# Gate and up projections of a decoder layer: stationary weights with 256 token columns moving, against stationary tokens with 512 weight columns moving

## The chip, the cores and the metric

The kernel runs on one core of a Trainium2 chip. The core has a matrix engine (TensorE, PE in the profile; its weight loads are PEld), a vector engine (VectorE, DVE), an activation engine (ScalarE, ACT), GpSimd (POOL), a queue engine (SyncE, SP), and DMA engines that move data between HBM and the on-chip memory SBUF. Matmul results land in PSUM, in 8 banks of 512 float32 columns on 128 partitions. The metric is device time of the whole launch in microseconds; lower is better.

## The reference, cut to what matters

One layer of a hybrid decoder on 256 tokens (plus 16 meta tokens), model width 2048, in float32. After the token mixers comes a SwiGLU feed-forward with hidden width 5632:

```python
def channel_mixing(h, w_gate_up, w_down, g_pre, g_post):
    xn = rmsnorm(h, g_pre)
    gu = jnp.einsum('bld,df->blf', xn, w_gate_up)
    gate, up = gu[..., :FFN_HIDDEN], gu[..., FFN_HIDDEN:]
    y = jnp.einsum('blf,fd->bld', jax.nn.silu(gate) * up, w_down)
    return rmsnorm(y, g_post)
```

Ahead of it stand the in-projection (2048 to 5132 columns), mLSTM, stick-breaking and pooling mixers, and the out-projection (2048 to 2048) with its norm and residual.

## The kernel before, in words

All large products run in a split form: each float32 operand is written as `hi` (rounded to the matrix engine's one-pass format fp32r) and `lo` (the rest), and a product is three matmuls, hi·hi, hi·lo and lo·hi. Weights are streamed from HBM in chunks of 1 MB into one of three `raw` buffers (`load`, L82); ScalarE makes `hi` (L93), VectorE makes `lo` (L94), each in two pieces of 1024 columns, into four `hi` and four `lo` buffers (`split`, L88). Loads are issued on SyncE's queue as a raw buffer comes free. A matmul has a stationary operand of 128x128 and a moving one of up to 512 columns. The program stands in the order in which the source issues it, and a scheduler then orders each engine's instructions by readiness and priority.

The stages, in order: in-projection (weights stationary, up to 272 token columns moving); out-projection in two halves (`ktile_product`, tokens stationary, 512 weight columns moving, L626 to L628); the first group of gate and up (512 gate and 512 up columns, `fg_part`, L738, tokens stationary, 512 columns moving, L744 to L746); ten more groups of gate and up (L826 to L851); the down projection in two halves (`ktile_product` again).

In those ten groups the weights are stationary and the 256 token columns `x2hi`, `x2lo` move (`mm3`, L97). A group has four blocks of 128 hidden columns, a PSUM bank each, gate in the left half and up in the right. The loop runs over four chunks `c` of 4 k tiles and over `s` (gate, up). The results have hidden channels on the partitions and tokens in the columns, which is what the down projection needs as its stationary operand. Each block is scaled by the second norm's factor per token column, `rb2`, and multiplied (L848 to L851) into float32 tiles `ha`, `hb`, `hc`. `rb2` is made in `norm2` with two float32 matmuls (L726). The first group has tokens on the partitions, so it uses the norm factor as a per-partition scalar (L769, L770) and is turned by eight TensorE transposes (L823) ahead of group 2.

In the down projection `lhs_h` (L868) splits each hidden k tile again, once per half, into `hh` and `hl` from a pool of six each (L872, L873).

Of the kernel before, what the change touches and what calls it, by code (L numbers as in the profile page):

```python
# [18 lines left out]
P = 128  # L19
D = 2048  # L20
# [17 lines left out]
def tile_hybrid_layer(  # L38
# [22 lines left out]
    cst = ctx.enter_context(tc.tile_pool(name="cst", bufs=1))  # L61
    wp = ctx.enter_context(tc.tile_pool(name="wp", bufs=1))
# [113 lines left out]
    # gate weights, input gate columns at 0..5 and forget gate columns at 32..37  # L176
# [290 lines left out]
    def tick():  # L467
        # one block's worth of matmuls has been issued: let one waiting step follow, if its input has had time
# [68 lines left out]
    def first(kind, i):  # L537
        # first token that a block is needed for
# [8 lines left out]
    def load_group(ka, kb, blocks):  # L547
        nb = len(blocks)
        starts = [base[kind] + P * i for kind, i in blocks]
        raw = wp.tile([P, 2 * MB], F32, tag="raw", name=nm("raw"), bufs=RAWB)  # L550
# [68 lines left out]
    mhi, mlo_ = mix_tiles()  # L619

    def ktile_product(wview, nk, half, accs, lhs, on_block, ticks=False, before_tail=None):
        # accs[i][j]: token tile i, 512-column block j of this half; the last four k tiles go block by block
# [8 lines left out]
        for ci in range(0, nk, 2):  # L631
# [3 lines left out]
            if ci + 4 < nk:  # L635
# [28 lines left out]
    def post_evac(accs, i, cb, yt, gt, ss):  # L664
# [4 lines left out]
        if cb == 2:  # L669
            # the mean square of the blocks so far, and EPS  # L670
# [17 lines left out]
    fp = ctx.enter_context(tc.tile_pool(name="fp", bufs=1))  # L688
    exst = ExitStack()
    ex = exst.enter_context(tc.tile_pool(name="ex", bufs=4))  # L690
    h2 = fp.tile([P, 2, D], F32, name="h2")
    gpost = fp.tile([P, D], F32, tag="gpost", name="gmp")
    act.dma_start(out=gpost, in_=g_mix_post.broadcast_to([P, D]))
    act.dma_start(out=h2, in_=x_v)
    yg = fp.tile([P, 2, D], F32, tag="yg", name="yg")
# [16 lines left out]
    rb2 = fp.tile([P, NT], F32, name="rb2")  # L712

    def norm2():
# [16 lines left out]
    fg_split, later = {}, []  # L731

    def fg_load(c, where=None):
        for s in range(2):
            r = load(gu_view(c * 4, s * HID), 4, 512)
            fg_split[s, c] = [(c * 4 + 2 * j, split(r[:, 2 * j : 2 * j + 2], 2, 512, where)) for j in range(2)]

    def fg_part(s, c, i):  # L738
        ts = slice(i * P, (i + 1) * P)
        for k0, (h, l) in fg_split[s, c]:  # L740
            for kk in range(2):
                k = k0 + kk
                o = fg_banks[s][i]
# [3 lines left out]

    fg_banks = []

    def fg_begin():  # L750
        four = [mx() for _ in range(4)]
        fg_banks.extend([four[s], four[s + 2]] for s in range(2))
        for s in range(2):
            fg_part(s, 0, 0)

    def fg_rest():
        for s in range(2):
            fg_part(s, 0, 1)
        norm2()
        exst.close()  # L760
        for c in range(1, 4):
            fg_load(c)
            for s in range(2):
                for i in range(2):
                    fg_part(s, c, i)
                    if c == 3 and s == 1:
                        sc = rr[:, 1, i : i + 1]
                        hg = fp.tile([P, 512], F32, tag="hg", name=nm("hg"), bufs=2)
                        act.activation(hg, fg_banks[0][i], AF.Silu, scale=sc)  # L769
                        vec.scalar_tensor_tensor(out=hg, in0=fg_banks[1][i], scalar=sc, in1=hg,  # L770
                                                 op0=ALU.mult, op1=ALU.mult)
                        later.append((i, hg))
# [7 lines left out]
    def finish_mix(i, j):  # L780
# [30 lines left out]
    ha = big.tile([P, 16, NT], F32, tag="mixhi", name="ha")  # L811
    hb = big.tile([P, 16, NT], F32, tag="mixlo", name="hb")
    hc = fw.tile([P, 12, NT], F32, tag="hc", name="hc", bufs=1)

    def hid(f):
        return ha[:, f, :] if f < 16 else hb[:, f - 16, :] if f < 32 else hc[:, f - 32, :]


    def first_group_end():
        for i, hg in later:  # L820
            pt = mx()
            for b in range(4):
                pe.transpose(pt[:, b * P : (b + 1) * P], hg[:, b * P : (b + 1) * P], ident)  # L823
            act.copy(out=ha[:, 0:4, i * P : (i + 1) * P], in_=pt.rearrange("p (a b) -> p a b", b=P))

    for gi in range(1, 11):  # L826
        if gi == 2:
            first_group_end()
        banks = [mx() for _ in range(4)] if gi % 2 == 0 else [acc(b) for b in range(4)]
        for c in range(4):  # L830
            for s in range(2):
                r = load(gu_view(c * 4, s * HID + gi * 512), 4, 512)
                subs = [(c * 4 + 2 * j, split(r[:, 2 * j : 2 * j + 2], 2, 512)) for j in range(2)]
                last = c == 3
                if last:
                    its = [(k0, kk, h, l, b) for b in range(4) for k0, (h, l) in subs for kk in range(2)]
                else:
                    its = [(k0, kk, h, l, b) for k0, (h, l) in subs for b in range(4) for kk in range(2)]
                for k0, kk, h, l, b in its:
                    k = k0 + kk  # L840
                    bs = slice(b * P, (b + 1) * P)
                    mm3(banks[b][:, s * NT : (s + 1) * NT], h[:, kk, bs], l[:, kk, bs], x2hi[:, k, :], x2lo[:, k, :],
                        k == 0 and s == 0, k == KT - 1, skip_group_check=True)
                    if last and s == 1 and k == KT - 1:
                        f = gi * 4 + b
                        t1 = fw.tile([P, NT], F32, tag="t1", name=nm("t1"))
                        t2 = fw.tile([P, NT], F32, tag="t2", name=nm("t2"))
                        vec.tensor_tensor(out=t1, in0=banks[b][:, :NT], in1=rb2, op=ALU.mult)  # L848
                        act.activation(t1, t1, AF.Silu)
                        vec.tensor_tensor(out=t2, in0=banks[b][:, NT:], in1=rb2, op=ALU.mult)  # L850
                        vec.tensor_tensor(out=hid(f), in0=t1, in1=t2, op=ALU.mult)  # L851

# [1 line left out]
    gpost2 = fp.tile([P, D], F32, tag="gpost", name="gfp")  # L854
    sp.dma_start(out=gpost2, in_=g_ffn_post.broadcast_to([P, D]))
# [66 lines left out]
```

## Time and profile before

| | |
|---|---|
| time, median of 3 runs | 1154.13 us (1154.11 to 1154.23) |
| span of the profiled execution | 1154.4 us |
| PE busy | 1143.4 us, 99%, 7795 matmuls |
| PEld busy | 1058.6 us, 92% |
| DVE, ACT busy | 677.2 us (59%), 519.4 us (45%) |
| DMA | 208.84 MB, mean 181 GB/s |

The profiled execution is one run of the program; its span, 1154.4 us, is 0.3 us over the median of the timed runs. A matmul's listed duration reaches from its start to a modelled end and contains its way through the array, so that several overlap; what a matmul costs is read from the distance between the starts of consecutive ones.

### The profile page before, as it was taken

The page shows a single profiled execution, that of the slowest core. Times are in us where ns is not written, and L with a number is a line of the kernel's source. Part 1 is how long each engine was busy: PE and PEld are TensorE (multiplying, and loading weights), DVE is VectorE, ACT ScalarE, POOL GpSimd, SP SyncE. Part 2 cuts the span into 40 slices and gives each one's busy share as a digit, 9 for nine tenths or more (in the row PEclk, how much of TensorE's full clock was granted, in tenths as well). Part 3 has the DMA queues.
Part 4 walks back from the last instruction along what each step waited for, and adds up shares of the span by engine and source line. Part 5 has one row for each costly group of instructions (what it writes and reads, how often), then busy time and mean ns, then how long its engine had stood idle before and what let it go on. Part 6 is the DMA issues. An engine that isn't in the chain of part 4 may idle for free.

```text
span 1154.4 us, 18718 instructions
## 1 busy us (share of the span) xinstructions
PE 1143.4 (99%) x7795; PEld 1058.6 (92%) x7795; DVE 677.2 (59%) x936; ACT 519.4 (45%) x759; POOL 23.0 (2%) x65
## 2 busy tenths in 40 slices
PE   9999999999999999999999999999999999999997
PEld 7999999999888789999999999999999888878885
DVE  4777655759945845645455365454453765565555
ACT  6544445534444844434334344343343544454442
POOL 4000000000000000000000000000000000000000
PEclk8999999999999999999999999999999999999999
DMA  7554543555465565455555554555555555555551
GB/s 237 179 181 149 188 146 114 170 147 170 167 273 219 183 208 193 167 188 184 179 189 183 185 183 167 202 183 177 190 183 184 185 182 183 183 187 193 195 190 73
DMA packets 100565, 208.84 MB, mean 181 GB/s; under 512 B 3962, under 2 KB 31402, under 8 KB 99952
## 3 DMA queue, kind: packets, MB, share of 16 engines
q1 hardware_dynamic: 99312, 202.63, 51.2%
q10 hardware_dynamic: 416, 3.15, 0.6%
q0 software_dynamic: 752, 1.87, 0.6%
q8 instruction: 61, 1.00, 0.4%
q14 instruction: 24, 0.20, 0.0%
HBM read 205.52 MB, written 2.11 MB: 180 GB/s over the span
## 4 chain that ended last, share of the span: by engine, by line
PE 98%; DVE 1%; DMA 0%; ACT 0%; issue 0%; SPq 0%; DVEq 0%; POOLq 0%; ACTq 0%
PE acc L100 14%; PE acc L98 14%; PE acc L99 14%; PE mx L98 7%; PE mx L100 7%; PE mx L99 7%; PE mx L627 5%; PE acc L627 5%; PE mx L628 5%; PE mx L626 5%; PE acc L628 5%; PE acc L626 5%; PE mx L744 1%; PE mx L746 1%; PE mx L745 1%; PE mx L327 0%
## 5 line engine op out<-in xcount | busy, mean ns | idle before, releaser
L94 DVE TENSOR_TENSOR lo<-raw,hi 128x1024 fp32r<-128x1024 f32 (+1 forms) x384 | 458.6, 1200 | 363.4 <-ACT hi L93 361.4
L93 ACT CAST hi<-raw 128x1024 fp32r<-128x1024 f32 (+1 forms) x384 | 391.7, 1029 | 398.4 <-PE acc L99 210.1
L100 PE MATMUL acc<-xhi,lo 128*128 128x272 f32 (+4 forms) x640 | 192.4, 301 | 0.0
L98 PE MATMUL acc<-xhi,hi 128*128 128x272 f32 (+4 forms) x640 | 187.7, 293 | 0.6 <-DVE im L292 0.4
L99 PE MATMUL acc<-xlo,hi 128*128 128x272 f32 (+4 forms) x640 | 187.1, 292 | 0.0
L98 PE MATMUL mx<-x2hi,hi 128*128 128x256 f32 x640 | 181.3, 283 | 0.0
L99 PE MATMUL acc<-x2lo,hi 128*128 128x256 f32 x640 | 181.1, 283 | 0.0
L100 PE MATMUL acc<-x2hi,lo 128*128 128x256 f32 x640 | 181.1, 283 | 0.0
L98 PE MATMUL acc<-x2hi,hi 128*128 128x256 f32 x640 | 181.1, 283 | 0.0
L99 PE MATMUL mx<-x2lo,hi 128*128 128x256 f32 x640 | 181.1, 283 | 0.0
L100 PE MATMUL mx<-x2hi,lo 128*128 128x256 f32 x640 | 181.1, 283 | 0.0
L98 PEld LDWEIGHTS acc<-xhi,hi 128*128 128x128 f32 x640 | 121.8, 190 | 2.7 <-issue 1.4
L100 PEld LDWEIGHTS acc<-xhi,lo 128*128 128x128 f32 x640 | 121.7, 190 | 1.6 <-issue 1.0
L98 PEld LDWEIGHTS mx<-x2hi,hi 128*128 128x128 f32 x640 | 122.9, 192 | 0.1
L99 PEld LDWEIGHTS acc<-x2lo,hi 128*128 128x128 f32 x640 | 122.9, 192 | 0.0
L98 PEld LDWEIGHTS acc<-x2hi,hi 128*128 128x128 f32 x640 | 122.9, 192 | 0.0
L100 PEld LDWEIGHTS acc<-x2hi,lo 128*128 128x128 f32 x640 | 122.9, 192 | 0.0
L99 PEld LDWEIGHTS mx<-x2lo,hi 128*128 128x128 f32 x640 | 122.9, 192 | 0.0
L100 PEld LDWEIGHTS mx<-x2hi,lo 128*128 128x128 f32 x640 | 122.9, 192 | 0.0
L99 PEld LDWEIGHTS acc<-xlo,hi 128*128 128x128 f32 x640 | 121.8, 190 | 0.5 <-DVE xlo L215 0.2
L627 PE MATMUL mx<-lo,hh 128*128 128x512 f32 x176 | 69.7, 396 | 0.0
L627 PE MATMUL acc<-lo,hh 128*128 128x512 f32 x176 | 69.6, 396 | 0.0
(246 smaller groups left out, 1390.8 us busy)
## 6 DMA issues: line engine op xcount, KB each, us to landing
raw<-in_w_gate_up_dram SPq DMA_DIRECT2D x88, 1024.0 KB, 4.9
raw<-in_w_down_dram SPq DMA_DIRECT2D x44, 1024.0 KB, 4.9
raw<-in_w_in_dram SPq DMA_DIRECT2D x36, 512.0 KB, 4.7
raw<-in_w_out_dram SPq DMA_DIRECT2D x16, 1024.0 KB, 5.0
raw<-in_w_in_dram SPq DMA_DIRECT2D x12, 1024.0 KB, 5.1
raw<-in_w_in_dram SPq DMA_DIRECT2D x8, 768.0 KB, 4.3
raw<-in_w_in_dram SPq DMA_DIRECT2D x3, 792.0 KB, 6.9
h<-in_x_dram ACTq DMA_DIRECT2D x1, 2048.0 KB, 11.9
```

What stands on the lines that cost most here:

```text
L93: act.copy(out=h, in_=r)
L94: vec.tensor_tensor(out=l, in0=r, in1=h.bitcast(F32), op=ALU.subtract)
L98: pe.matmul(o, lhsT=wh, rhs=xh, start=start, stop=False, **kw)
L99: pe.matmul(o, lhsT=wh, rhs=xl, start=False, stop=False, **kw)
L100: pe.matmul(o, lhsT=wl, rhs=xh, start=False, stop=stop, **kw)
L626: pe.matmul(o, lhsT=lh, rhs=h[:, 0, js], start=k == 0, stop=False)
L627: pe.matmul(o, lhsT=lh, rhs=l[:, 0, js], start=False, stop=False)
L628: pe.matmul(o, lhsT=ll, rhs=h[:, 0, js], start=False, stop=k == nk - 1)
L744: pe.matmul(o, lhsT=x2hi[:, k, ts], rhs=h[:, kk, :], start=k == 0, stop=False)
L745: pe.matmul(o, lhsT=x2hi[:, k, ts], rhs=l[:, kk, :], start=False, stop=False)
L746: pe.matmul(o, lhsT=x2lo[:, k, ts], rhs=h[:, kk, :], start=False, stop=k == KT - 1)
```

## The change

All eleven groups now run as the first one did: tokens stationary, 512 weight columns moving (`gu_part`), gate and up for each of the two token tiles in a bank of their own. `gu_evac` takes Silu of the gate bank with the norm factor as scale and multiplies it with the up bank into `hg`, tokens on partitions. After the next group's first chunk, `hidden_out` transposes a group's `hg` by eight TensorE transposes into two spare banks, ScalarE copies them out as `hi`, VectorE writes `lo`; these stay in SBUF (`hidhi`, `hidlo`), and `lhs_h` only picks slices. `rb2` and its matmuls are gone. The last group's transposes stand in the down projection after its first chunk of weights.

The second part is where tiles lie in SBUF. Pools stack from the low end in the order in which they are opened; `rawp` and `ft` (for `hg`) are now on the right side, at the high end. Counted from the tiles' sizes, in KB (1024 bytes) of a partition:

| tiles | before | after |
|---|---|---|
| raw | 17 to 41 | 200 to 224 |
| hi, lo (weights) | 41 to 57, 57 to 73 | 17 to 33, 33 to 49 |
| x2hi, x2lo (and xhi, xlo) | 73 to 90, 90 to 107 | 49 to 66, 66 to 83 |
| mixhi, mixlo (out-projection) | 107 to 123, 123 to 139 | 83 to 99, 99 to 115 |
| hi, lo of the first group's first chunk | 186 to 202, 202 to 218 | 157 to 173, 173 to 189 |
| stationary tiles of down, hi | hh 206 to 212 | groups 0 to 3: 83 to 99, 4 to 10: 133 to 161 |
| stationary tiles of down, lo | hl 212 to 218 | groups 0 to 3: 99 to 115, 4 to 10: 161 to 189 |

The core of the diff:

```diff
+    rawp = ctx.enter_context(tc.tile_pool(name="rawp", bufs=1, side="right"))
...
-        raw = wp.tile([P, 2 * MB], F32, tag="raw", name=nm("raw"), bufs=RAWB)
+        raw = rawp.tile([P, 2 * MB], F32, tag="raw", name=nm("raw"), bufs=RAWB)
...
-        pr = acc(3)
-        for i in range(2):
-            dg = fp.tile([P, P], F32, tag="dg", name=nm("dg"))
-            vec.tensor_scalar(out=dg, in0=ident, scalar1=rr[:, 1, i : i + 1], scalar2=None, op0=ALU.mult)
-            pe.matmul(pr[:, i * P : (i + 1) * P], lhsT=ones, rhs=dg, start=True, stop=True)
-        vec.tensor_copy(out=rb2, in_=pr[:, :NT])
...
+    def gu_part(banks, s, i, subs):
+        ts = slice(i * P, (i + 1) * P)
+        for k0, (h, l) in subs:
+            for kk in range(2):
+                k = k0 + kk
+                o = banks[s][i]
+                pe.matmul(o, lhsT=x2hi[:, k, ts], rhs=h[:, kk, :], start=k == 0, stop=False)
+                pe.matmul(o, lhsT=x2hi[:, k, ts], rhs=l[:, kk, :], start=False, stop=False)
+                pe.matmul(o, lhsT=x2lo[:, k, ts], rhs=h[:, kk, :], start=False, stop=k == KT - 1)
+
+    def gu_evac(banks, i):
+        sc = rr[:, 1, i : i + 1]
+        hg = ft.tile([P, 512], F32, tag="hg", name=nm("hg"))
+        act.activation(hg, banks[0][i], AF.Silu, scale=sc)
+        vec.scalar_tensor_tensor(out=hg, in0=banks[1][i], scalar=sc, in1=hg, op0=ALU.mult, op1=ALU.mult)
+        return hg
...
+        for i, hg in enumerate(hgs):
+            pt = bank(i)
+            for b in range(4):
+                pe.transpose(pt[:, b * P : (b + 1) * P], hg[:, b * P : (b + 1) * P], ident)
+            p4 = pt.rearrange("p (a b) -> p a b", b=P)
+            ts = slice(i * P, (i + 1) * P)
+            act.copy(out=hidden[0][gi][:, :, ts], in_=p4)
+            vec.tensor_tensor(out=hidden[1][gi][:, :, ts], in0=p4, in1=hidden[0][gi][:, :, ts].bitcast(F32),
+                              op=ALU.subtract)
...
-    for gi in range(1, 11):
-        if gi == 2:
-            first_group_end()
-        banks = [mx() for _ in range(4)] if gi % 2 == 0 else [acc(b) for b in range(4)]
-        for c in range(4):
...
-                    mm3(banks[b][:, s * NT : (s + 1) * NT], h[:, kk, bs], l[:, kk, bs], x2hi[:, k, :], x2lo[:, k, :],
-                        k == 0 and s == 0, k == KT - 1, skip_group_check=True)
...
+    for gi in range(11):
+        banks = fg_banks if gi == 0 else four(gi)
+        hgs = []
+        for c in range(1 if gi == 0 else 0, 4):
             for s in range(2):
+                subs = gu_load(c, gi, s)
+                if c == 3:
+                    for i in range(2):
+                        gu_part(banks, s, i, subs)
+                        if s == 1:
+                            hgs.append(gu_evac(banks, i))
                 else:
+                    for sub in subs:
+                        for i in range(2):
+                            gu_part(banks, s, i, [sub])
+            if c == 0:
+                hidden_out(gi - 1, later, spare(gi - 1))
+        later = hgs
...
-                act.copy(out=hh, in_=hid(k))
-                vec.tensor_tensor(out=hlo, in0=hid(k), in1=hh.bitcast(F32), op=ALU.subtract)
...
+            return hidden[0][k // 4][:, k % 4, ts], hidden[1][k // 4][:, k % 4, ts]
```

Two smaller edits go with it: the last norm's gain `gfp` is loaded on POOL's queue into the space of `x2lo` (before: on SyncE's queue into a tile of its own), and the last result tile `yg2` lies in the space of `x2hi`.

PE, before, where the first group's transposes stand between group 1 (banks `acc`) and group 2 (banks `mx`); the names are output bank, then moving and stationary operand:

```order
L98 MATMUL acc_575_4481<-x2hi_3746,hi_614_4894 128x256
L99 MATMUL acc_575_4481<-x2lo_3747,hi_614_4894 128x256
L100 MATMUL acc_575_4481<-x2hi_3746,lo_615_4895 128x256
L823 MATMUL mx_624_4970<-ident_72,hg_570_4454 128x128 x4
L823 MATMUL mx_625_4976<-ident_72,hg_571_4469 128x128 x4
L98 MATMUL mx_626_4982<-x2hi_3746,hi_631_4988 128x256
L99 MATMUL mx_626_4982<-x2lo_3747,hi_631_4988 128x256
```

PE, after, at the end of group 1's first chunk; eight transposes of the group ahead stand here, and the same again in each later group and once in the down projection:

```order
L738 MATMUL acc_572_4479<-hi_581_4520,x2hi_3755 128x512
L739 MATMUL acc_572_4479<-lo_582_4521,x2hi_3755 128x512
L740 MATMUL acc_572_4479<-hi_581_4520,x2lo_3756 128x512
L764 MATMUL mx_583_4550<-ident_75,hg_567_4458 128x128 x4
L764 MATMUL mx_584_4557<-ident_75,hg_568_4473 128x128 x4
L738 MATMUL acc_569_4476<-hi_586_4566,x2hi_3755 128x512
L739 MATMUL acc_569_4476<-lo_587_4567,x2hi_3755 128x512
```

The weights have gone from the second place (stationary) to the first (moving), and one matmul of 512 columns does what two of 256 did. Up to the first group's second chunk the order on PE is the same in both programs.

VectorE, after, at the end of group 0 and the start of group 1 (the `lo` rows are pieces of group 1's weights; the two `hg` rows read group 0's up banks for token tiles 0 and 1):

```order
L96 TENSOR_TENSOR lo_575_4483<-raw_573_4480,hi_574_4482 128x1024
L96 TENSOR_TENSOR lo_577_4487<-raw_573_4480,hi_576_4486 128x1024
L746 SCALAR_TENSOR_TENSOR hg_567_4458<-mx_519_4124,rr_3737,hg_567_4458 128x512
L96 TENSOR_TENSOR lo_580_4517<-raw_578_4514,hi_579_4516 128x1024
L746 SCALAR_TENSOR_TENSOR hg_568_4473<-mx_520_4125,rr_3737,hg_568_4473 128x512
L96 TENSOR_TENSOR lo_582_4521<-raw_578_4514,hi_581_4520 128x1024
```

Three of the next group's four `lo` pieces stand ahead of the second `hg` row, which waits for the group's last matmul.

## Rows read from the trace of the kernel before

**Rows 1.** Busy time by stage: us, then PE, PEld, DVE, ACT, POOL; clock; DMA share; GB/s.

```profile
299.70:391.30 91.60, 91.25 (x409) 74.63 (x408) 58.21 (x79) 44.21 (x63) 0.56 (x1) 1.00 0.65 241
409.80:437.80 28.00, 28.00 (x125) 23.21 (x125) 13.28 (x13) 12.88 (x13) 0.00 (x0) 1.00 0.53 181
437.80:899.60 461.80, 461.80 (x3849) 461.65 (x3848) 236.54 (x284) 182.13 (x207) 0.00 (x0) 1.00 0.53 183
899.60:1146.60 247.00, 246.97 (x1058) 197.56 (x1056) 148.14 (x188) 119.48 (x183) 0.54 (x1) 1.00 0.50 177
1146.60:1154.40 7.80, 0.00 (x0) 0.00 (x0) 3.50 (x6) 0.69 (x2) 0.54 (x1) 0.84 0.44 162
```

**Rows 2.** The chain of work that ended last, by engine.

```profile
PE 98%; DVE 1%; DMA 0%; ACT 0%; issue 0%; SPq 0%; DVEq 0%; POOLq 0%; ACTq 0%
```

**Rows 3.** Timeline of PE in the ten groups: start us, us; nine steps apart.

```profile
559.80 0.28 PE L98 MATMUL acc<-x2hi,hi 128*128 128x256 f32 x1
...
560.88 0.28 PE L98 MATMUL acc<-x2hi,hi 128*128 128x256 f32 x1
```

**Rows 4.** Timeline of PE in the first group's later chunks, nine steps apart.

```profile
423.78 0.39 PE L745 MATMUL mx<-lo,x2hi 128*128 128x512 f32 x1
...
425.82 0.39 PE L745 MATMUL mx<-lo,x2hi 128*128 128x512 f32 x1
```

**Rows 5.** The same, where its first chunk ends and the second begins.

```profile
402.80 0.40 PE L746 MATMUL mx<-hi,x2lo 128*128 128x512 f32 x1
...
404.43 0.40 PE L744 MATMUL mx<-hi,x2hi 128*128 128x512 f32 x1
404.66 0.39 PE L745 MATMUL mx<-lo,x2hi 128*128 128x512 f32 x1
...
406.48 0.39 PE L744 MATMUL mx<-hi,x2hi 128*128 128x512 f32 x1
```

**Rows 6.** Timeline of PE in the down projection, nine steps apart.

```profile
999.74 0.40 PE L626 MATMUL acc<-hi,hh 128*128 128x512 f32 x1
...
1001.84 0.39 PE L626 MATMUL acc<-hi,hh 128*128 128x512 f32 x1
```

**Rows 7.** Timeline of PE around the first group's transposes.

```profile
483.91 1.03 PE L823 MATMUL mx<-ident,hg 128*128 128x128 f32 x8
484.70 0.36 PE L98 MATMUL mx<-x2hi,hi 128*128 128x256 f32 x1
484.90 0.28 PE L99 MATMUL mx<-x2lo,hi 128*128 128x256 f32 x1
```

**Rows 8.** Line 823 by itself: duration ns min/median/max, first and last start.

```profile
L823 PE MATMUL mx<-ident,hg x8: 271/272/273, 483.9 to 484.7; 128*128 128x128 f32 x8
```

**Rows 9.** Timeline of PE around four transposes among 512-column products.

```profile
387.19 0.60 PE L798 MATMUL acc<-ident,h 128*128 128x128 f32 x4
387.55 0.48 PE L626 MATMUL mx<-hi,mixhi 128*128 128x512 f32 x1
387.87 0.60 PE L798 MATMUL acc<-ident,h 128*128 128x128 f32 x4
```

**Rows 10.** Timeline of PE around the second norm's matmuls.

```profile
408.75 0.38 PE L726 MATMUL acc<-dg,ones 128*128 128x128 f32 x2
...
409.58 0.49 PE L726 MATMUL acc<-dg,ones 128*128 128x128 f32 x2
...
410.14 0.39 PE L745 MATMUL mx<-lo,x2hi 128*128 128x512 f32 x1
```

**Rows 11.** Groups on ACT and DVE: busy us, mean ns, idle before.

```profile
L93 ACT CAST hi<-raw 128x1024 fp32r<-128x1024 f32 x352 | 365.4, 1047 | 369.4 <-PE acc L99 187.3 <-PE mx L99 119.9 <-PE mx L628 19.7
L769 ACT ACTIVATE hg<-mx,rr 128x512 f32<-128x512 f32 x2 | 1.4, 690 | 0.0
L94 DVE TENSOR_TENSOR lo<-raw,hi 128x1024 fp32r<-128x1024 f32 x352 | 428.3, 1223 | 347.1 <-ACT hi L93 346.6
L770 DVE SCALAR_TENSOR_TENSOR hg<-mx,rr,hg x2: 745/745/745, 435.5 to 438.9; 128x512 f32<-128x512 f32 x2
```

More of the change, by code (lines that the diff above doesn't have):

```diff
@@ L549, in load_group @@
         starts = [base[kind] + P * i for kind, i in blocks]
-        raw = wp.tile([P, 2 * MB], F32, tag="raw", name=nm("raw"), bufs=RAWB)
+        raw = rawp.tile([P, 2 * MB], F32, tag="raw", name=nm("raw"), bufs=RAWB)
         r = raw[:, : (kb - ka) * nb * P].rearrange("p (k c) -> p k c", c=nb * P)
@@ L642, in ktile_product @@
                 pend = []
+            if ci == 0 and after_first:
+                after_first()
         if before_tail:
@@ L688, in tile_hybrid_layer @@
     fp = ctx.enter_context(tc.tile_pool(name="fp", bufs=1))
+    ft = ctx.enter_context(tc.tile_pool(name="ft", bufs=4, side="right"))
     exst = ExitStack()
+    yp = exst.enter_context(tc.tile_pool(name="yp", bufs=1))
     ex = exst.enter_context(tc.tile_pool(name="ex", bufs=4))
     h2 = fp.tile([P, 2, D], F32, name="h2")
-    gpost = fp.tile([P, D], F32, tag="gpost", name="gmp")
+    gpost = yp.tile([P, D], F32, name="gmp")
     act.dma_start(out=gpost, in_=g_mix_post.broadcast_to([P, D]))
     act.dma_start(out=h2, in_=x_v)
-    yg = fp.tile([P, 2, D], F32, tag="yg", name="yg")
+    yg = yp.tile([P, 2, D], F32, name="yg")
     ssy = fp.tile([P, 2, 4], F32, name="ssy")
@@ L709, in gu_view @@
         return w_gu[0, k0 * P : (k0 + 4) * P, c0 : c0 + 512].rearrange("(k p) c -> p k c", p=P)
-    rb2 = fp.tile([P, NT], F32, name="rb2")
     def norm2():
@@ L721, in norm2, with gu_load @@
             inv_rms(rr[:, 1, i : i + 1], s1, 1)
-        pr = acc(3)
-        for i in range(2):
-            dg = fp.tile([P, P], F32, tag="dg", name=nm("dg"))
-            vec.tensor_scalar(out=dg, in0=ident, scalar1=rr[:, 1, i : i + 1], scalar2=None, op0=ALU.mult)
-            pe.matmul(pr[:, i * P : (i + 1) * P], lhsT=ones, rhs=dg, start=True, stop=True)
-        vec.tensor_copy(out=rb2, in_=pr[:, :NT])
[L731 to L738, printed above, removed]
+    def gu_load(c, gi, s, where=None):
+        r = load(gu_view(c * 4, s * HID + gi * 512), 4, 512)
+        return [(c * 4 + 2 * j, split(r[:, 2 * j : 2 * j + 2], 2, 512, where)) for j in range(2)]
+    def gu_part(banks, s, i, subs):
         ts = slice(i * P, (i + 1) * P)
-        for k0, (h, l) in fg_split[s, c]:
+        for k0, (h, l) in subs:
             for kk in range(2):
                 k = k0 + kk
-                o = fg_banks[s][i]
+                o = banks[s][i]
                 pe.matmul(o, lhsT=x2hi[:, k, ts], rhs=h[:, kk, :], start=k == 0, stop=False)
@@ L746, in fg_part, with hidden_out @@
                 pe.matmul(o, lhsT=x2lo[:, k, ts], rhs=h[:, kk, :], start=False, stop=k == KT - 1)
-    fg_banks = []
+    def gu_evac(banks, i):
[4 more added lines that the diff above has]
+        return hg
+    hidden = []
+    def hidden_out(gi, hgs, bank):
+        if gi < 8 and gi % 4 == 0:
+            for s in ("hi", "lo"):
+                if gi == 0:
+                    q = big.tile([P, 16, NT], F32R, tag=f"mix{s}", name=f"hid{s}")
+                    hidden.append([q[:, 4 * g : 4 * g + 4] for g in range(4)])
+                else:
+                    q = hp.tile([P, 28, NT], F32R, name=f"hid{s}2")
+                    hidden[s == "lo"] += [q[:, 4 * g : 4 * g + 4] for g in range(7)]
+        for i, hg in enumerate(hgs):
[7 more added lines that the diff above has]
+                              op=ALU.subtract)
@@ L750, in fg_begin, with four, spare @@
+    fg_split, later = {}, []
+    fg_banks = []
+    def four(gi):
+        f = [mx() for _ in range(4)] if gi % 2 == 0 else [acc(b) for b in range(4)]
+        return [f[0:2], f[2:4]]
+    def spare(gi):
+        return (lambda i: mx()) if gi % 2 == 0 else acc
     def fg_begin():
-        four = [mx() for _ in range(4)]
-        fg_banks.extend([four[s], four[s + 2]] for s in range(2))
+        fg_banks.extend(four(0))
         for s in range(2):
-            fg_part(s, 0, 0)
+            gu_part(fg_banks, s, 0, fg_split[s])
@@ L756, in fg_rest @@
     def fg_rest():
         for s in range(2):
-            fg_part(s, 0, 1)
+            gu_part(fg_banks, s, 1, fg_split[s])
         norm2()
         exst.close()
[L761 to L772, printed above, removed]
@@ L804, in finish_mix @@
                                          in1=x2hi[:, k, ts].bitcast(F32), op0=ALU.mult, op1=ALU.subtract)
-    ktile_product(wout_view, KT, 1, accs1, lhs_mix, done, before_tail=lambda: fg_load(0, ex))
+    ktile_product(wout_view, KT, 1, accs1, lhs_mix, done, before_tail=lambda: fg_split.update((s, gu_load(0, 0, s, ex)) for s in range(2)))
     fg_rest()
-    fw = ctx.enter_context(tc.tile_pool(name="fw", bufs=4))
-    ha = big.tile([P, 16, NT], F32, tag="mixhi", name="ha")
-    hb = big.tile([P, 16, NT], F32, tag="mixlo", name="hb")
@@ L813, in tile_hybrid_layer @@
[L813 to L824, printed above, removed]
-    for gi in range(1, 11):
-        if gi == 2:
-            first_group_end()
-        banks = [mx() for _ in range(4)] if gi % 2 == 0 else [acc(b) for b in range(4)]
-        for c in range(4):
-            for s in range(2):
[L832 to L836, printed above, removed]
-                else:
[L838 to L841, printed above, removed]
-                    mm3(banks[b][:, s * NT : (s + 1) * NT], h[:, kk, bs], l[:, kk, bs], x2hi[:, k, :], x2lo[:, k, :],
-                        k == 0 and s == 0, k == KT - 1, skip_group_check=True)
[L844 to L851, printed above, removed]
@@ L854, in tile_hybrid_layer @@
-    gpost2 = fp.tile([P, D], F32, tag="gpost", name="gfp")
-    sp.dma_start(out=gpost2, in_=g_ffn_post.broadcast_to([P, D]))
-    yg2 = fp.tile([P, 2, D], F32, tag="yg", name="yg2")
+    hp = ctx.enter_context(tc.tile_pool(name="hp", bufs=1))
+    for gi in range(11):
+        banks = fg_banks if gi == 0 else four(gi)
+        hgs = []
+        for c in range(1 if gi == 0 else 0, 4):
+            for s in range(2):
+                subs = gu_load(c, gi, s)
[4 more added lines that the diff above has]
+                            hgs.append(gu_evac(banks, i))
+                else:
+                    for sub in subs:
[4 more added lines that the diff above has]
+        later = hgs
@@ L857, in tile_hybrid_layer @@
+    gpost2 = big.tile([P, KT * T], F32, tag="xlo", name="gfp")[:, :D]
+    pool.dma_start(out=gpost2, in_=g_ffn_post.broadcast_to([P, D]))
+    yg2 = big.tile([P, KT * T], F32, tag="xhi", name="yg2")[:, : 2 * D].rearrange("p (i d) -> p i d", d=D)
     ssz = fp.tile([P, 2, 4], F32, name="ssz")
@@ L865, in tile_hybrid_layer, with lhs_h @@
         accs = [flat[0:2], flat[2:4]]
-        hl = {}
-        def lhs_h(k, i, hl=hl):
-            if k not in hl:
-                hh = fw.tile([P, NT], F32R, tag="hh", name=nm("hh"), bufs=6)
-                hlo = fw.tile([P, NT], F32R, tag="hl", name=nm("hl"), bufs=6)
-                act.copy(out=hh, in_=hid(k))
-                vec.tensor_tensor(out=hlo, in0=hid(k), in1=hh.bitcast(F32), op=ALU.subtract)
-                hl[k] = (hh, hlo)
+        def lhs_h(k, i):
             ts = slice(i * P, (i + 1) * P)
-            return hl[k][0][:, ts], hl[k][1][:, ts]
+            return hidden[0][k // 4][:, k % 4, ts], hidden[1][k // 4][:, k % 4, ts]
         def done2(i, j, half=half, accs=accs):
@@ L890, in finish_ffn @@
                 sp.dma_start(out=out_v[:, i, cs], in_=yg2[:, i, cs])
-        ktile_product(wd_view, NF, half, accs, lhs_h, done2)
+        last = (lambda: hidden_out(10, later, spare(10))) if half == 0 else None
+        ktile_product(wd_view, NF, half, accs, lhs_h, done2, after_first=last)
 _INS = ['x', 'meta_tokens', 'w_in', 'ml_conv_w', 'ml_igate_b', 'ml_fgate_b', 'pool_w', 'pool_scale', 'w_out',
```

2 lines of the change are left out of this document (1 added, 1 removed).

## The prediction

> **What bounds the kernel now.** I read the busy times by stage first. In the ten groups of gate and up PE is busy for 461.80 of 461.80 us, in the down projection for 246.97 of 247.00, in the out-projection for 91.25 of 91.60, while DVE and ACT are busy for 237 and 182 us of the 461.8 [rows 1]. Then the chain that ended last: PE has 98% of it [rows 2]. So PE never waits for data in the stages that the change touches, and their length is the number of matmuls times the distance between two starts. That distance is the number to read; the listed 0.28 and 0.39 us of one matmul overlap.
>
> The timeline gives it. 256 moving columns: nine steps in 560.88 - 559.80 = 1.08 us, 120 ns each [rows 3]. The stage agrees: (461.8 us - 0.87 for the eight transposes inside it) / 3840 products = 120.0 ns. 512 columns in the first group: nine steps in 425.82 - 423.78 = 2.04 us, 226.7 ns [rows 4]. 512 in the down projection: 1001.84 - 999.74 = 2.10 us, 233.3 ns [rows 6], and the stage 247.0 / 1056 = 233.9. At the granted clock of 1.00 in these stages [rows 1], the 2.4 GHz level, 512 columns are 213.3 ns and 256 are 106.7. So each matmul pays a fixed 13.3 ns in both of the first cases, whichever of weights and tokens is stationary, and 20 ns in the down projection.
>
> Where do the other 6.7 ns come from? In the first group the first chunk's `hi` and `lo` lie at 186 to 218 KB, the later chunks' at 41 to 73. Between 402.80 and 404.43 seven steps take 233 ns each; from 404.66, the second matmul that reads the low buffers, to 406.48 eight take 227.5 [rows 5]. Same instructions, same stationary tiles; the place of the moving tile is what differs. In the down projection it is the stationary tile that lies high (206 to 218 KB), with all else at or below 73. The out-projection, with stationary tiles at up to 139 KB, is a 512-column stage without the high ones. I take it that an operand high in SBUF costs 6.7 ns per matmul. One switch carries this, so it stays a reading.
>
> **The ten groups' products.** 10 groups x 2 (gate, up) x 4 blocks x 16 k tiles x 3 = 3840 matmuls become 10 x 2 x 2 token tiles x 16 x 3 = 1920. New operands lie at 17 to 49 and 49 to 83 KB. 3840 x 120.0 = 460.9 us; 1920 x 226.7 = 435.3. Change: -25.6 us, all on the path. If the high spacing came instead, 1920 x 233.3 = 447.9: -13.0.
>
> The Trainium skill, "TensorE: Matmul & The Clock Gate", section "Back-to-back issue gap", gives the distance of two matmuls at the full clock as N/2.4 + 2.5 ns. By it a fixed part of 2.5 ns would be saved 1920 times, an estimate of 4.8 us. Rows 3 and 4 show 13.3 in its place, and the sum goes by them.
>
> **The transposes.** 80 more on PE (8 for each of groups 1 to 10; group 0's were there). Nothing hides them: PE is the bound. Eight took 483.91 to 484.70, and the product behind them had a step of 0.20 us for 0.12 [rows 7]: 0.79 + 0.08 = 0.87 us. Among 512-column products four took 0.36 and the next step 0.32 for 0.23 [rows 9], 0.45 us; eight in one piece are then 8 x 0.099 + 0.09 = 0.88. 10 x 0.87 = +8.7 us. After such an interruption some ten steps run nearer to 233 than to 227 (the same is seen behind the norm's matmuls): 10 x 0.04 = +0.4. Lower end 8.4, upper 10 x 0.45 x 2 plus twice that tail, 9.8.
>
> A single transpose is listed with 272 ns [rows 8], and they start 99 ns apart. The Trainium skill, same page, section "Part 4: PE-mode transpose", has about 275 ns for one in a kernel. The duration agrees with that; taken as a cost, 80 of them would be an estimate of 22 us, but the path pays the spacing [rows 7].
>
> They wait for `hg`, which needs Silu and one multiply after the group's last matmul, 0.69 + 0.745 us [rows 11], and they stand 48 matmuls, 10.9 us, behind it. So no wait is added there.
>
> **The norm's matmuls.** From 408.75 to 410.14, 1.39 us, PE does four float32 matmuls and three products [rows 10]; three products alone are 0.68. Change: -0.7.
>
> **The down projection.** 1056 matmuls, 233.9 ns now. All low: 1056 x 6.9 = -7.3. Only k tiles 0 to 15 certainly low (83 to 115 KB): 16/44 of that, -2.6. Unknown is the stretch between 139 KB, the highest low tile seen, and 186, the lowest high one. `hidhi` of the later groups, 133 to 161, is nearer to the first, `hidlo`, 161 to 189, to the second. `lo` of 28 k tiles is read by 28 x 8 = 224 matmuls; the other 832 x 6.9 = -5.7. I take that. If the 20 ns came instead from the waits on `hh` and `hl`, which also go, it would be -7.3; if from something that stays, 0.
>
> **Costed at nothing.** DVE: per group 16 operations on 256 columns become two multiplies of 0.745 us and two subtractions on 512; per 1024-column piece of weights it has 1.22 us of work [rows 11] against 12 x 0.227 = 2.72 us of PE time, ACT 1.05. The `lhs_h` work of the down projection goes; both were covered. The one new wait that could reach PE is on DVE: the multiply for token tile 1 waits for the group's last matmul, with the fourth `lo` piece of the next group behind it. That piece is ready 0.745 + 1.22 = 2.0 us after the group's end and is wanted after three pieces, 8.2 us. The copies of a transposed group wait on ACT and DVE for PE's transposes, with splits behind them that are wanted a chunk, 5.4 us, later. Loads: PE now eats 1 MB in 24 x 0.227 = 5.4 us for 5.8, 193 GB/s for 183; the out-projection ran 241 [rows 1]. The `gfp` load moves from SP's queue, where weight loads stood behind it, to POOL's, where it waits for the last read of `x2lo` with only the final norm's two powers behind it, and is wanted 120 us later. In-projection and out-projection move down by 24 KB inside the low stretch: 0. The first chunk of the first group, 48 matmuls, moves from 186 to 218 to 157 to 189: 0, at most -0.3. The tail of 7.8 us [rows 1] keeps its work.
>
> **Sum.** -25.6 + 8.7 + 0.4 - 0.7 - 5.7 = -22.9 us. The profiled execution's span of 1154.4 becomes 1131.5; it stands 0.3 over the median, so the time is 1131.2 us.
>
> **Rivals.**
> - *The gain is in the ten groups alone.* The down projection keeps 233 ns, because what is high there is not what costs, or the boundary lies just over 139 KB: -17.2 to -19.8, 1134 to 1137 us. For it: the boundary has not been seen. Against: the sharp switch in rows 5. 18%.
> - *The spacing is 233 everywhere.* The extra 6.7 ns then belongs to something the change carries into the ten groups. 1131.2 + 12.9 + 5.7 = 1149.8. Against: 227 for the same instruction on the same stationary tiles [rows 4]. 8%.
> - *PE waits at every group boundary.* All `lo` pieces of the next group come late behind the new multiply: 0.745 + 1.22 = 2.0 us each, after which DVE's 1.22 per piece outruns PE's 2.72. 10 x 2.0: 1151. Against: the order has three pieces ahead of it. 3%.
> - *Slower: the fixed part is small and the transposes outweigh it.* The place is the stream of products: halving their number gives back only the fixed part, 1920 times, and the transposes cost 9.1. The point from which it decides is 9.1/1920 = 4.7 ns. If 512 columns cost twice what 256 do (240 ns), halving gives back nothing, and with the down projection as it was the time is 1154.1 + 9.1 - 0.7 = 1162.5 us. Against it stand rows 3 and 4, 13.3 ns in both forms [rows 3, 4]. 4%. The rule of the Trainium skill's "TensorE: Matmul & The Clock Gate" cited above lies on this side of the point: its 2.5 ns would make an estimate of 1157.7.
> - *A further step lower.* Operands below 41 KB save another 6.7 ns in the in-projection (1920 matmuls), out-projection (384) and gate and up (2112): -29.6, 1102 us. For it: the step from 20 to 13.3. Against: 13.3 is the same with tiles at 41 and at 139 KB. 3%.
>
> **How the numbers follow.** Forecast 64%: 1131.2, by its bounds (down -7.3 to -2.6, transposes 8.4 to 9.8) 1129 to 1135. With the first rival 82%, so the range is 1126 to 1141: at the low end all of the down projection (-1.6) and 3.5 us for stages costed at nothing, at the high end no gain there (1137) and 4 us more for transposes or short waits. 0.2%, 2.3 us, is what a measurement of this kernel can tell from no change. Faster: 64 + 18 + 3, 7 of the 8 and 2 of the 3: 94%. Same: 2%. Slower: 4%.
>
> **What would show it.** PE timeline in groups 1 to 10: steps of 226.7 ns, eight transposes at 0.87 us once a group, no wait of PE on DVE or ACT; gate and up from group 1 on about 444 us. In the down projection, steps of 227 for k tiles 0 to 15, and from 16 on 227 for the two matmuls that hold `hidhi` and about 233 for the one with `hidlo`. In-projection unchanged to 0.5 us. The prediction is wrong where the 512-column steps in the ten groups differ from 227 by more than 3 ns, or where PE shows waits of over 0.5 us per group.

## The result, and the profile after

The changed kernel takes 1134.97 us, median of 4 runs (1134.61 to 1135.14), against 1154.18 us for the kernel before (1154.11 to 1154.6). The ratio is 0.9834, 95% interval 0.9822 to 0.9846: 19.2 us less, where 22.9 were forecast (1131.2 us).

Busy time by stage in the kernel after: out-projection, first group, ten groups, down projection, end. Columns as in [rows 1].

```profile
298.16:389.65 91.49, 91.14 (x408) 74.56 (x407) 58.10 (x79) 43.95 (x63) 0.56 (x1) 1.00 0.68 241
389.65:435.43 45.78, 45.78 (x209) 37.47 (x208) 28.18 (x52) 28.34 (x59) 2.53 (x3) 1.00 0.45 142
435.43:879.70 444.27, 444.27 (x2002) 368.65 (x2000) 220.49 (x201) 189.93 (x200) 0.00 (x0) 1.00 0.58 190
879.70:1124.80 245.10, 245.10 (x1065) 198.42 (x1063) 114.45 (x105) 94.33 (x101) 1.14 (x2) 1.00 0.55 183
1124.80:1132.90 8.10, 0.17 (x1) 0.00 (x0) 3.50 (x6) 0.69 (x2) 0.54 (x1) 0.79 0.45 166
```

PE is busy for all of the three changed stages, as before [rows 1]. Against before, from the first matmul of each to the first of the next stage (the last one: to one step behind its last matmul), the ten groups went from 461.80 to 444.27 us, the first group from 46.54 to 45.78, the down projection from 246.76 to 245.11 with eight transposes more in it, the out-projection from 91.53 to 91.49.

All waits of PE in the kernel after: who waited, for what, us in total, times, longest.

```profile
PE mx L212 <- DMA mt<-in_meta_tokens_dram: 1.7, 1, 1.7
PE mx L188 <- DVE ssx L200: 1.1, 1, 1.1
PE acc L100 <- DVE im L294: 0.4, 1, 0.4
PE acc L817 <- issue: 0.4, 1, 0.4
```

None stands in the ten groups or the down projection (L212, L188, L100 are the in-projection, L817 the turning of the out-projection's result). Now the starts of consecutive matmuls. PE in the ten groups of the kernel after, nine steps apart, then around one group's transposes (start us, us, engine, line, tile, shape):

```profile
560.10 0.39 PE L739 MATMUL acc<-lo,x2hi 128*128 128x512 f32 x1
...
562.14 0.39 PE L739 MATMUL acc<-lo,x2hi 128*128 128x512 f32 x1
```

```profile
446.32 1.03 PE L764 MATMUL mx<-ident,hg 128*128 128x128 f32 x8
447.11 0.48 PE L738 MATMUL acc<-hi,x2hi 128*128 128x512 f32 x1
447.42 0.39 PE L739 MATMUL acc<-lo,x2hi 128*128 128x512 f32 x1
```

2.04 us / 9 = 226.7 ns, the spacing of [rows 4] carried to all groups. The eight transposes take 0.79, the next step 0.31 for 0.23: 0.87 us, as [rows 7] gave. PE in the down projection of the kernel after, in the third block of four k tiles and in the fifth, nine steps each:

```profile
902.37 0.39 PE L628 MATMUL acc<-hi,hidhi 128*128 128x512 f32 x1
...
904.40 0.39 PE L628 MATMUL acc<-hi,hidhi 128*128 128x512 f32 x1
...
924.13 0.39 PE L628 MATMUL acc<-hi,hidhi 128*128 128x512 f32 x1
...
926.23 0.40 PE L628 MATMUL acc<-hi,hidhi 128*128 128x512 f32 x1
```

2.03 / 9 = 226 ns for k tiles up to 15, 2.10 / 9 = 233 ns from 16 on, for all three matmuls of a k tile. The prediction wanted 227 for the two that hold `hidhi`. That is the main step that failed, and most of the experiments are about it.

### The profile page after: what moved, and what is told of

Same layout as the page of the kernel before. It is cut to its first block, busy times and chain, and to the rows that moved or that the text cites. A ratio compares the mean times of both kernels' runs of the same rounds, so it can differ in the third digit from the quotient of the medians.

```text
span 1132.9 us, 14585 instructions
## 1 busy us (share of the span) xinstructions
PE 1121.4 (99%) x5951; PEld 964.8 (85%) x5951; DVE 626.5 (55%) x767; ACT 501.5 (44%) x671; POOL 22.8 (2%) x66
## 4 chain that ended last, share of the span: by engine, by line
PE 98%; DVE 1%; DMA 0%; ACT 0%; issue 0%; SPq 0%; DVEq 0%; POOLq 0%; ACTq 0%
PE mx L738 8%; PE mx L740 8%; PE mx L739 8%; PE acc L102 7%; PE acc L100 7%; PE acc L101 7%; PE acc L739 6%; PE acc L740 6%; PE acc L738 6%; PE mx L629 5%; PE acc L629 5%; PE mx L630 5%; PE mx L628 5%; PE acc L630 5%; PE acc L628 5%; PE mx L764 0%
## 5 line engine op out<-in xcount | busy, mean ns | idle before, releaser
L100 PE MATMUL acc<-xhi,hi 128*128 128x272 f32 (+4 forms) x640 | 187.1, 292 | 0.4 <-DVE im L294 0.4
L738 PE MATMUL mx<-hi,x2hi 128*128 128x512 f32 x384 | 150.1, 391 | 0.0
L740 PE MATMUL mx<-hi,x2lo 128*128 128x512 f32 x384 | 149.7, 390 | 0.0
L739 PE MATMUL mx<-lo,x2hi 128*128 128x512 f32 x384 | 149.5, 389 | 0.0
L738 PE MATMUL acc<-hi,x2hi 128*128 128x512 f32 x320 | 124.9, 390 | 0.0
L740 PE MATMUL acc<-hi,x2lo 128*128 128x512 f32 x320 | 124.6, 389 | 0.0
L739 PE MATMUL acc<-lo,x2hi 128*128 128x512 f32 x320 | 124.5, 389 | 0.0
L100 PEld LDWEIGHTS acc<-xhi,hi 128*128 128x128 f32 x640 | 121.5, 190 | 2.2 <-issue 1.4
L740 PEld LDWEIGHTS mx<-hi,x2lo 128*128 128x128 f32 x384 | 72.1, 188 | 15.0
L738 PEld LDWEIGHTS mx<-hi,x2hi 128*128 128x128 f32 x384 | 72.1, 188 | 14.9 <-ACT x2hi L821 0.2
L739 PEld LDWEIGHTS mx<-lo,x2hi 128*128 128x128 f32 x384 | 72.1, 188 | 14.7
L629 PE MATMUL mx<-lo,hidhi 128*128 128x512 f32 x176 | 69.4, 394 | 0.0
```

Source lines behind the costliest of these rows:

```text
L100: pe.matmul(o, lhsT=wh, rhs=xh, start=start, stop=False, **kw)
L629: pe.matmul(o, lhsT=lh, rhs=l[:, 0, js], start=False, stop=False)
L738: pe.matmul(o, lhsT=x2hi[:, k, ts], rhs=h[:, kk, :], start=k == 0, stop=False)
L739: pe.matmul(o, lhsT=x2hi[:, k, ts], rhs=l[:, kk, :], start=False, stop=False)
L740: pe.matmul(o, lhsT=x2lo[:, k, ts], rhs=h[:, kk, :], start=False, stop=k == KT - 1)
```

## The experiments

The theory on record: a matmul of 512 columns costs 6.7 ns more where an operand lies high in SBUF. Rivals: the down projection waited on `hh` and `hl`; or something else in the address decides.

**Is the height worth anything?** `e1_raw_low` puts the raw buffers of the kernel after back to the low end, so that every operand of the products lies 24 KB higher. `e2_layout_only` does the other half: the kernel before with its raw buffers at the high end.

```diff
# e1, on the kernel after
-    rawp = ctx.enter_context(tc.tile_pool(name="rawp", bufs=1, side="right"))
+    rawp = wp
# e2, on the kernel before (the change of `raw` stands in two places)
+    rawp = ctx.enter_context(tc.tile_pool(name="rawp", bufs=1, side="right"))
-        raw = wp.tile([P, 2 * MB], F32, tag="raw", name=nm("raw"), bufs=RAWB)
+        raw = rawp.tile([P, 2 * MB], F32, tag="raw", name=nm("raw"), bufs=RAWB)
```

> The changed kernel with the raw buffers back at the low end, so that every operand of TensorE lies 24 KB higher than in the changed kernel: weights' hi and lo at 41 to 73 KB, x2 at 73 to 107, hidden groups 0 to 3 at 107 to 139, groups 4 to 10 at 157 to 213. Theory A (a matmul costs 6.7 ns more when an operand lies above a boundary between 139 and 161 KB, and nothing else of the place matters): steps of 226.7 ns in gate and up and for k tiles 0 to 15 of the down projection, 233 for 16 to 43, the same time as the changed kernel within 1 us. Theory B (the lower the operands, the shorter the step): gate and up slower by some of 2112 x 6.7 = 14 us. Theory C (the boundary moved down with the layout, it is a distance between operands): k tiles 0 to 15 stay at 227 as well, so A and C agree here and B stands apart.

> The kernel before with only the raw buffers moved to the high end, so that all other tiles lie 24 KB lower; hh and hl of the down projection come to 182 to 194 KB (before: 206 to 218). Theory A: hh and hl are still above the boundary, so the down projection keeps 233 ns a matmul and the time stays at 1154 us within 1 us. Theory B: every stage is a little shorter, 1140 to 1150 us.

e1: 1134.42 us (ratio 0.9827, 0.9812 to 0.9842), gate and up 490.04 us and down 245.09 against 490.05 and 245.11 after. e2: 1153.97 (1.0001, 0.9992 to 1.001), down 246.78. So moving the raw buffers, and everything else by 24 KB with them, is worth nothing in either kernel; the gain lies in the rest of the change.

**Waits or place?** `e3_hh_low` is the kernel before with `hh` and `hl` in rings inside `xhi` and `xlo`, whose tiles are dead by then (73 to 107 KB). The copies and the waits on them stay.

```diff
+    hx = [big.tile([P, KT * T], F32R, tag=t, name=f"{t}_h") for t in ("xhi", "xlo")]
...
-                hh = fw.tile([P, NT], F32R, tag="hh", name=nm("hh"), bufs=6)
-                hlo = fw.tile([P, NT], F32R, tag="hl", name=nm("hl"), bufs=6)
+                q = k % 6
+                hh = hx[0][:, q * NT : (q + 1) * NT]
+                hlo = hx[1][:, q * NT : (q + 1) * NT]
```

> The kernel before with one edit: hh and hl, the stationary tiles of the down projection, lie at 73 to 107 KB in the space of x2 in place of 206 to 218; they are still made anew for each k tile, in rings of six, and PE still waits for them. Theory A (the place costs): down projection at 226.7 ns a matmul, 239.5 us for 247, time 1147 us. Rival (the waits on tiles made just before cost): 233 ns as before, 1154 us.

1149.51 us (0.9957, 0.994 to 0.9974). PE's longest waits in e3, and its down projection, nine steps:

```profile
PE mx L626 <- ACT xhi_h L874: 1.2, 1, 1.2
...
PE acc L626 <- ACT xhi_h L874: 0.8, 1, 0.8
```

```profile
985.37 0.39 PE L626 MATMUL acc<-hi,xhi_h 128*128 128x512 f32 x1
...
987.41 0.39 PE L626 MATMUL acc<-hi,xhi_h 128*128 128x512 f32 x1
```

227 ns with the copies still there: the waits are refuted. The rings cost two waits instead, 2.0 us together, most of the 2.5 by which the time falls short of the 1147 expected. This looked like height, until the next one.

**Where is the boundary?** `e4_interleave` lays groups 4 to 10 of the kernel after group by group, `hi` beside `lo`, from 133 KB up.

```diff
-                    q = hp.tile([P, 28, NT], F32R, name=f"hid{s}2")
-                    hidden[s == "lo"] += [q[:, 4 * g : 4 * g + 4] for g in range(7)]
+                    if s == "hi":
+                        for g in range(4, 11):
+                            for j, s2 in enumerate(("hi", "lo")):
+                                hidden[j].append(hp.tile([P, 4, NT], F32R, name=f"hid{s2}{g}"))
```

> The changed kernel with the hidden tiles of groups 4 to 10 laid out group by group, hi and lo side by side, 8 KB a group, from 133 KB up to 189 (in the changed kernel all hi at 133 to 161 and all lo at 161 to 189). Theory A, with lo above the boundary slowing the two matmuls beside it: the groups switch from 227 to 233 ns a matmul one after the other, and the first slow group shows the boundary; groups 4 and, if the boundary is near 160 KB, 5 and 6 run at 227: 1.3 to 4 us faster than the changed kernel. Rival (the boundary lies under 133 KB, and 13.3 ns in the out-projection before at 123 to 139 KB has another reason): all seven groups at 233, the same time. Rival (no boundary, something of groups 4 to 10 other than the place): all at 233, the same time.

1134.33 us (0.9826, 0.9811 to 0.9841). PE in e4, k tiles 12 to 15 and 16 to 19 of the first half, 48 matmuls each (stretch, us, PE busy, clock, DMA share, GB/s):

```profile
912.85:923.74 10.89, 10.89 (x49) 1.00 0.61 196
923.74:934.94 11.20, 11.20 (x49) 1.00 0.56 191
```

The step is there from the first tile at 133 KB, with no way through from 227 to 233 at a height; and in e1 `hidlo` of groups 0 to 3 lies at 123 to 139 KB and is fast. PE in e1, k tiles 14 and 15, nine steps:

```profile
919.52 0.39 PE L628 MATMUL acc<-hi,hidhi 128*128 128x512 f32 x1
...
921.56 0.39 PE L628 MATMUL acc<-hi,hidhi 128*128 128x512 f32 x1
```

Both 133 to 139 KB fast and 133 to 141 KB slow can't be a matter of height. What the slow pairs share is smaller: counted from the tiles' sizes, weights, `x2` and the pool `fp` start at 32 bytes past a multiple of 64, but the small tiles of `fp` add up to an odd multiple of 32, so that the pools behind it start at a multiple of 64. In bytes, start of the stationary tile minus start of the moving one, mod 256: 0 in every fast stage (the ten groups, the first group's later chunks, k tiles 0 to 15, e3); 224 for `hh` and `hl` before and for k tiles 16 to 43 after; 32 in the first group's first chunk.

**The relative start.** `e7_pad32` adds 32 unused bytes to the kernel after, at the start of `fp`. `e8_all_at_0` puts 32 bytes ahead of everything else too, so that the operands of all products start at multiples of 64 and still agree.

```diff
# e7 and e8, on the kernel after
+    fp.tile([P, 8], F32, name="pad32")
# e8 alone
+    cst.tile([P, 8], F32, name="pad32c")
```

> The changed kernel with one unused tile of 32 bytes at the start of the pool that holds the late tiles, so that the hidden tiles of groups 4 to 10 and the first group's first hi and lo start at 32 bytes past a multiple of 64, as all other fp32r operands do; they stay at the same KB. New theory D (a matmul costs 6.7 ns more when its moving and stationary operand do not start at the same place within 64 bytes; all steps of 227 seen so far are of 32 with 32, all of 233 of 0 with 32): down projection at 227 for all k tiles, 28/44 x 1056 x 6.8 = -4.6 us against the changed kernel, 1130.2 us. Theory A (the height in SBUF): no change, 1134.6 us.

> The one before with a second unused tile of 32 bytes at the very start, so that every fp32r operand starts at a multiple of 64. Theory D (the two must agree): as with both at 32, 1130 us. Theory E (an operand at a multiple of 64 is slow, at 32 fast): 233 ns everywhere, 2112 x 6.7 = +14 us in gate and up, +7 in the down projection, +2.6 in the out-projection, 1154 us or more.

e7: 1130.50 us (1130.33 to 1131.11; 0.9801, 0.9787 to 0.9814). e8: 1130.42 (0.9801, 0.9788 to 0.9814), down 240.87. PE in e7, at the fifth block of k tiles, nine steps:

```profile
924.23 0.39 PE L628 MATMUL acc<-hi,hidhi 128*128 128x512 f32 x1
...
926.27 0.39 PE L628 MATMUL acc<-hi,hidhi 128*128 128x512 f32 x1
```

227 ns where the kernel after has 233; the down projection takes 240.89 us for 245.11. That is 4.2 us from 32 bytes that hold nothing, at heights up to 189 KB. e8 says that it is the difference of the two starts and not where each stands.

**The same on the kernel before.** `e11_before_pad32` is the one line of e7 on the kernel before; `hh` and `hl` stay at 206 to 218 KB.

> The kernel before with one unused tile of 32 bytes at the start of the pool that holds hh and hl (and the first group's first chunk of weights). They stay at 206 to 218 KB (and 186 to 218), only 32 bytes higher, and their starts then agree with the weights' in 256 bytes. If the relative start decides: down projection at 226.7 ns a step, 1056 x 6.7 = 7.1 us less, 239.7 us, and the first group's first chunk at 227 as well (48 x 6.7 = 0.3 us), time 1154.1 - 7.4 = 1146.7. If the height in SBUF decides, as the prediction read it: no change, 1154. If the waits on hh and hl decide: no change, 1154.

1147.96 us (1147.02 to 1150.05; 0.995, 0.9933 to 0.9967). PE in e11: gate and up, then the down projection.

```profile
388.86:897.19 508.33, 508.33 (x4061) 1.00 0.53 182
897.19:1137.32 240.13, 240.13 (x1058) 1.00 0.51 181
```

240.13 us, 239.7 expected. The 0.3 us expected of the first chunk of weights does not come: gate and up take 508.33 for 508.34. Its first ten steps do fall from 233 ns (391.30 to 393.63 us before) to 227 (388.86 to 391.13); the others stand behind transposes, where the steps are uneven in both. Against the kernel before in its own job, e7 takes 23.2 us less (1153.66 there) and e11 6.7 less (1154.62): with all starts in agreement the change is worth -16.5 us. The terms that are not the down projection's summed to -17.2, and later first loads (see below) take back 0.8.

**How much of the address must agree?** `e9_offsets` gives each of groups 4 to 10 an offset of its own; by the tiles' sizes `hi` comes to lie at distances 0, 64, 240, 16, 232, 228 and 24, and `lo` 128 further. `e10_same_offset` does so with `hi` and `lo` of a group at the same distance.

```diff
# e10, on the kernel after
-                    q = hp.tile([P, 28, NT], F32R, name=f"hid{s}2")
-                    hidden[s == "lo"] += [q[:, 4 * g : 4 * g + 4] for g in range(7)]
+                    if s == "hi":
+                        q = hp.tile([P, 56 * NT + 448], F32R, name="hid2")
+                        at = 0
+                        for d in (128, 64, 192, 16, 240, 112, 8):
+                            at += (8 + d // 4 - at) % 64
+                            for j in range(2):
+                                hidden[j].append(q[:, at : at + 4 * NT].rearrange("p (a b) -> p a b", b=NT))
+                                at += 4 * NT
```

> The changed kernel with the hidden tiles of groups 4 to 10 laid out group by group, each started at its own offset within 128 bytes: group 4 at 32, 5 at 96, 6 at 16, 7 at 48, 8 at 8, 9 at 4, 10 at 56; the moving weights stay at 32. Theory D with blocks of 64 bytes: groups 4 and 5 at 227 ns. If it is the half of 64 bytes that must agree: 48 and 56 fast as well, 16, 8 and 4 slow. If the exact offset must agree: 16, 48, 8, 4 and 56 all slow, perhaps by other amounts. Theory A: all seven at 233.

> The kernel after, with the hi and lo of hidden groups 4 to 10 laid out group by group, both of a group at the same distance from the weights (start of the stationary tile minus start of the moving tile, taken mod 256 bytes): 128, 64, 192, 16, 240, 112, 8. In the run before, one group mixed two distances, so that it stayed open how much of the address must agree. If the two starts must agree in 256 bytes: all seven groups step by more than 227 ns per matmul. If in 128: the first of the seven steps by 226.7, the other six by more. If in 64: the first three (128, 64, 192) step by 226.7, the other four by more. A slow group has 96 matmuls at 6.7 ns, 0.64 us, so the times lie close together, 1130.5 us plus 4.5 (256), 3.9 (128) or 2.6 (64): 1135.0, 1134.4, 1133.1, and it is read from the steps. Groups 0 to 3 (distance 0) 226.7 in each case.

e9 ran 1133.56 us and e10 1133.8, one run each. In e9 no group came to 227: 229.0 to 233.3 in the mean, so agreement within 64 bytes, which would have made the first two fast, is not enough. In the group whose `hi` is at distance 0 and `lo` at 128 only the first of the three matmuls took 226.6 ns. The second, `hi` with the weights' `lo`, agrees in its own two starts too and took 232.5; the matmul behind it is the first with the stationary tile at 128. So a matmul's own two starts are not all that counts; whether it is the next one's stationary tile was not tried by itself. PE in e10, groups 3 to 9 in the first half (distances 0, 128, 64, 192, 16, 240, 112), 48 matmuls a row:

```profile
913.61:924.50 10.89, 10.89 (x50) 1.00 0.58 194
924.50:935.65 11.15, 11.15 (x49) 1.00 0.58 193
935.65:946.85 11.20, 11.20 (x49) 1.00 0.56 188
946.85:957.85 11.00, 11.00 (x50) 1.00 0.57 190
957.85:969.05 11.20, 11.20 (x49) 1.00 0.56 189
969.05:980.03 10.98, 10.98 (x50) 1.00 0.57 191
980.03:991.22 11.19, 11.19 (x49) 1.00 0.58 191
```

All six lie over the first row's 10.89, and group 10 steps by 231.0 ns: of the three readings only 256 bytes is left. The cost is not all or nothing, and it does not simply grow with the distance: 228.7 ns at 240 (16 short of agreement), 229.1 at 192, but 233.3 at 224 in the kernel after, and 233.4 at 16 and at 64. Why is open.

**Are the transposes on the path?** `e6_transposes_twice` does each group's eight twice, 88 more.

```diff
-            for b in range(4):
+            for b in (0, 1, 2, 3, 0, 1, 2, 3):
```

> The changed kernel with each of its 88 transposes done twice (the same values again), to price them. By the rows: 88 x 0.099 = +8.7 us, and no wait, since the copies have slack. If they were hidden: 0. If a transpose cost its listed 0.272 us: +24.

1144.38 us (0.9919, 0.9906 to 0.9933), 9.4 over after where 8.7 were expected. PE in e6, around one group's:

```profile
446.31 1.91 PE L764 MATMUL mx<-ident,hg 128*128 128x128 f32 x16
447.98 0.48 PE L738 MATMUL acc<-hi,x2hi 128*128 128x512 f32 x1
```

1.67 us for 0.79: 0.107 us a transpose over the whole run, all of it in the time, with no new wait.

## Why the prediction was right, and where it was not

- **The ten groups' products** (-25.6) and **the transposes** (+8.7, +0.4): right. Forecast 444.4 us for the stage, measured 444.27; steps 226.7 ns, 0.87 us per eight. e6 shows the transposes' cost directly. The fixed part is 13.3 ns in the new form too, and the rival that rested on a small fixed part fell. The Trainium skill ("TensorE: Matmul & The Clock Gate", "Back-to-back issue gap") calls its N/2.4 + 2.5 ns the gap of an isolated matmul, and gives about 131 ns per matmul for a stream of 512 columns; the prediction took the first for a stream. No stream here shows either: it steps by 226.7 ns.
- **The norm's matmuls** (-0.7): -0.76.
- **Covered work and waits** (0): right; no wait of PE in the changed stages.
- **The down projection** (-5.7): this step failed by its size. It measured 245.11 - 246.76 - 0.88 for the eight transposes = -2.5 us, about the bound given for k tiles 0 to 15 alone (-2.6). The step read [rows 5] as a matter of height and so placed `hidhi` on the fast side. [rows 5] show the same matmul at two relative starts, 32 and 0 bytes mod 256, as well as at two heights, and one switch couldn't tell them apart. e4 refuted height, e7, e8 and e11 showed the start. The first rival's clause, that what is high is not what costs, was the right one, and 1134.97 lies in its 1134 to 1137 us as well as at the upper end of the forecast's 1129 to 1135. That k tiles 0 to 15 ran at 227 as forecast was luck: not because they lie low, but because the tiles that they took over from the out-projection start where the weights do, mod 256 bytes.
- **Unchanged stages** (0): the in-projection came out another way. The next two rows are PE's first transpose of the meta tokens, before and then after, with the wait ahead of it.

```profile
5.34 0.23 PE L210 MATMUL mx<-ident,mt 16*128 16x16 f32 x1 [0.21 <-DMA mt<-in_meta_tokens_dram]
```

```profile
6.83 0.28 PE L212 MATMUL mx<-ident,mt 16*128 16x16 f32 x1 [1.70 <-DMA mt<-in_meta_tokens_dram]
```

The load is issued at 1.73 us in both and lands 3.6 us later before, 5.0 after. The first product starts at 8.72 before and 9.88 after. So it does in every kernel of the new form (9.45 to 9.93) against every one of the old (8.38 to 8.72), wherever the raw buffers lie. By the end of the in-projection 0.8 us of it is left (298.16 against 297.37 in e11; over all pairs of profiled executions of the two forms, the long one of the kernel before aside, it is 0.3 to 1.4). Why the first loads land later was not tried.

The sum: 3.2 (down) + 0.8 (first loads) - 0.2 (ten groups and norm) = 3.8 us, what lies between 1131.2 and 1134.97. The two spans, 1154.4 and 1132.9, differ by 21.5 and not by 19.2, and the granted clock goes with it. Stretch 10 to 100 us, before and then after (columns as in [rows 1]):

```profile
10.00:100.00 90.00, 89.62 (x684) 84.82 (x683) 62.32 (x112) 48.92 (x97) 6.59 (x31) 0.95 0.56 179
```

```profile
10.00:100.00 90.00, 89.62 (x701) 85.54 (x700) 64.74 (x117) 50.18 (x99) 5.79 (x28) 1.00 0.60 188
```

The granted clock was 0.95 there in the profiled execution of before, which ended its in-projection at 299.77 us; e2, e3 and e11, with the same in-projection, end it at 297.1 to 297.4. That one execution was some 2 us long, and the time of a run stands 1.7 us over its span (1134.61 and 1132.9). The prediction took the 0.3 between span and median as all there was; the two errors cancel in the sum.

The best kernel is e7, the kernel after with the 32 bytes: 1130.50 us.

## What to carry to other kernels

Where PE is the bound, read the spacing of the starts, not the durations: halving the number of matmuls gives back their fixed part (13.3 ns here), and extra transposes cost their spacing (0.1 us). When a spacing differs between two stretches, list everything that differs in their addresses before naming one, and try the cheapest (here 32 unused bytes) alone.

## What the runs showed of the hardware that was not expected

A 512-column matmul took 226.7 ns where the stationary and the moving tile start at the same place mod 256 bytes, and 228.7 to 233.4 in the groups of e10 where they don't. In e7 the two starts of groups 4 to 10 are 256 apart mod 512 and the spacing is 226.7, so agreement in 256 is enough there. The height in SBUF, up to 218 KB (e11), made no difference.

This is shown for 512 columns with the tokens stationary, and it does not carry over to the in-projection (weights stationary, 272 columns moving). There `xhi` and `xlo` have 1088 bytes a k tile, so the distance goes through 0, 192, 128 and 64 from one k tile to the next, and steps at 0 are not the shortest. In the kernel after, from 110 us on, the 272-column matmuls of this stage step by 126.2, 125.2, 127.3 and 124.6 ns in the mean (171 to 190 steps each, those over 140 ns left out). Three steps at 64, then three at 0:

```profile
138.35 0.29 PE L100 MATMUL acc<-xhi,hi 128*128 128x272 f32 x1
...
138.72 0.29 PE L100 MATMUL acc<-xhi,hi 128*128 128x272 f32 x1
...
139.10 0.29 PE L100 MATMUL acc<-xhi,hi 128*128 128x272 f32 x1
```
